# A router that takes its root by log and exp, and experts that fetch their tokens by row: one change to a two-layer transformer kernel

## Chip, core and metric

The kernel runs on one core of a Trainium2 chip. The metric is the device time of one execution in microseconds (us); three runs of the kernel before took 1812.9, 1816.25 and 1819.8, median 1816.25. All data are f32 in DRAM.

## What is computed

One sequence of 512 tokens with 1024 features goes through two blocks. The first has a mixer (a recurrence and attention, with 256 context tokens), then a layer of 16 experts; the second has another mixer and a wide feed-forward layer. The change lies at the seam of the first mixer and the experts. The reference there, cut down:

```python
x = x + g1 * y_x                                  # y_x ends with ... @ w_out
h = modulate(rms_norm(x, norm2_g), sh2, sc2)      # h * (1 + sc2) + sh2
aff = softmax(h @ w_router)                       # 512 x 16
gate, idx = top_k(swapaxes(aff, 1, 2), 64)        # each expert takes its 64 best tokens
xe = h[idx]
hid = silu(xe @ w_gate) * (xe @ w_up)             # per expert, 64 x 1024
ye = (hid @ w_down) * gate
x = x + g2 * zeros_like(h).at[idx].add(ye)
```

Each expert has three weights of 1024 x 1024, so the 16 experts read 201 MB.

## The kernel before

**Tools.** The kernel is written in a tile language: pools hand out buffers by tag and count, and the waits are made from the reads and writes of the tiles. The language also sets the order of the instructions on each engine with a timing model of its own, so an engine's order can differ from the order of the lines; `after` adds an order by hand. A product of f32 operands leaves two records in the trace, a transpose one. The products marked mm3 split f32 into a high and a low part (fp32r) and make three products of them.

**Output projection, mix_out (L937).** w_out is read in four blocks of 256 columns (loop n over wN). For each block and each of the four blocks b of 128 tokens, the result is scaled by g1 and added to X (L966, L967), and the squares of the row are summed on ACT (L968). `logits(n)` transposes two chunks of 128 features of all tokens (L955), scales them by sc2 on ACT (L957) and multiplies them with the router's weights into four accumulators lg (L959). It is called for block n - 1 within block n, and for the last block after the loop.

**Router (L982).** The row sums give 1/rms by `rstd` (L143): a square root on ACT, a reciprocal on DVE. Then a preload of the table for exp, the softmax over 16 columns, a transpose to 16 rows of 512 (L1004), eight rounds of max and match_replace (L1012, L1013) that mark the 64 best, a scan that numbers them (L1016), and a transpose back (L1020). `sl` then holds for each token and expert the slot 1 to 64, or 0.

**Experts, moe (L1024).** The experts go in eight pairs p; the two of a pair use the two halves of the array's columns (64 tokens each), so their products run side by side. Per pair:
- `gemm` (L1074) makes G with w_gate and U with w_up, from xe (chunks of 128 features x 128 chosen tokens); the weights come by `mload`.
- `back(p)` (L1114) makes the one-hot D by comparing iota with sl, transposes it (L1119), rounds it to fp32r as oh, and multiplies D with the affinities (L1124) for the gates gc.
- `prep(p + 1)` (L1097) scales a one-hot by 1/rms and gathers the next pair's tokens as a product of X with it (L1105), 8 chunks x 4 token blocks; the results get sc2 and sh2 on ACT and DVE (L1107, L1110). prep(0) stands before the first gemm.
- silu(G) * U is transposed (L1150), `gemm` makes Y with w_down, Y is scaled by gate and g2 and split in two fp32r parts yh (L1173 to L1175), and each of the four token blocks gets its scatter: two products with oh (L1178, L1179) and one addition on DVE (L1184) to an accumulator ACC. ACC is added to X on POOL at the last pair (L1171), whose scatter goes to X itself. The last pair makes Y in three column parts (`gemm_parts`, L1062).

**Weights.** `mload` (L1035) issues every load on SP's queue, in order; a load waits until its buffer's last reader is done, and the loads behind it wait too. A load is 1 MiB: chunks of 128 rows x 1024 columns, each partition getting pieces of 4 KB. The list `kinds` names the ring of buffers, 15 (x1 six times, raw 3, hl 3 as pairs of halves, x2 3); six more fresh buffers (the tags of rw1 and rw2, and the two of the accumulators) are used once before the ring goes round. The first loads are issued while mix_out runs.

Of the kernel before, what the change touches and what calls it, by code (L numbers as in the profile page):

```python
# [9 lines left out]
F32 = mybir.dt.float32  # L10
# [10 lines left out]
def constants():  # L21
# [31 lines left out]
    iota = np.repeat(np.arange(1, 65, dtype=f)[None, :], 128, axis=0)  # L53
    return {
# [6 lines left out]
    }  # L61

# [6 lines left out]
class Build:  # L69
# [111 lines left out]
    def first_mixer(self):  # L181
# [19 lines left out]
        at = 0  # L201
# [12 lines left out]
        put("n2", I["norm2_g"][0].rearrange("(r p) -> r p", p=128), 8)  # L214
# [12 lines left out]
        nc.vector.tensor_copy(self.pcol, tp[:, :128])  # L227
        cs = p1.tile([128, 8, 32], F32, name="cs")
# [157 lines left out]
        es1.close()  # L386
        esw = ExitStack()
# [20 lines left out]
    def ctx_part(self, cx, rest):  # L408
# [20 lines left out]
        def shift(i):  # L429
            for j, at in enumerate((0, 1, 2, 3)):  # L430
                if at == i:
                    self.mod_col(cx, pc, (self.sh2, self.sc2)[j // 2], 3 + j // 2, j % 2)
# [18 lines left out]
        nc.vector.scalar_tensor_tensor(self.sc2, self.sc2, 1.0, self.c("n2"), op0=ALU.add, op1=ALU.mult)  # L451
# [473 lines left out]
    def mod_col(self, pool, psp, out, wi, half, tag="mr"):  # L925

        nc = self.nc
        for s, row in self.mod_rows(pool, psp, wi, tag, (half,)):
            ps = psp.tile([128, 512], F32, name="mr", tag=tag, bufs=self.nmr)
            for k in range(4):  # L930
                nc.tensor.matmul(ps[:, 2 * k:2 * k + 2], row[:, k * 128:(k + 1) * 128], self.selc,
                                 start=True, stop=True)
            c = 8 * wi + 4 * s
            nc.vector.tensor_tensor(out[:, 4 * s:4 * s + 4], ps[:, :8].rearrange("p (k i) -> p k i", i=2)[:, :, 0],
                                    self.c("bmod")[:, c:c + 4], op=ALU.add)

    def mix_out(self, end):  # L937
# [3 lines left out]
        nc.sync.dma_start(wr, I["w_router"][0].rearrange("(k p) e -> p k e", p=128))  # L941
# [9 lines left out]
        def logits(n):  # L951
            for k in (2 * n, 2 * n + 1):
                tp = pp.tile([128, 512], F32, name="tp", tag="tp", bufs=2)
                for b in range(4):
                    nc.tensor.transpose(tp[:, b * 128:(b + 1) * 128], self.X[:, b, k * 128:(k + 1) * 128], self.ident)  # L955
# [4 lines left out]

        for n, ks in enumerate(self.wN(I["w_out"][0], 0, 1024)):
            s = slice(n * 256, (n + 1) * 256)
            for b in range(4):
# [18 lines left out]
    def router(self):  # L982

        nc, mo, ms, pp = self.nc, self.mo, self.ms, self.pmx
        iota = self.iota = ms.tile([128, 64], F32, name="iota")
        nc.sync.dma_start(iota, self.I["k_iota"])
        rs = self.rs = ms.tile([128, 4], F32, name="rs")
# [3 lines left out]
        e = self.aff = ms.tile([128, 4, 16], F32, name="aff")  # L991
# [32 lines left out]
    def moe(self):  # L1024
# [4 lines left out]
        acc = [(self.mwx2, "acc0"), (self.mwx2, "acc1")]  # L1029
        kinds = ["x1"] * 6 + ["raw"] * self.nraw + ["hl"] * (self.nhl // 2) + ["x2"] * 3  # L1030
        self.tail = False
        todo = (kinds[:6] + [(self.rw1, "rw2"), (self.rw2, "rw")] + kinds[6:] +
                [(self.rw1, "rw"), (self.rw2, "rw2")] + acc)

        def mload(src, last):  # L1035
            if last == 2 and not self.tail:

                self.tail = True
                todo[:] = ["x2", "x2", "x2", (self.rw2, "rw2")] * 3
            if not todo:  # L1040
                todo.extend(k for k in kinds if not last or k != "hl")
            kind = todo.pop(0)
            shape = [128, src.shape[1], src.shape[2]]
# [12 lines left out]
            else:  # L1056
                pool, n = (self.mwx, 6) if kind == "x1" else (ms, 3)
                t = pool.tile(shape, F32, name="mwt", tag="mwt", bufs=n)
# [3 lines left out]
        def gemm_parts(ps, lhs, wa, wb):  # L1062

            ws = [w.rearrange("(k p) f -> p k f", p=128) for w in (wa, wb)]
            for y, c in zip(ps, parts):
                for kk in range(2):
                    tl = [mload(w[:, 4 * kk:4 * kk + 4, c], 2) for w in ws]
# [6 lines left out]
        def gemm(ps, lhs, wa, wb, last=0):  # L1074
            wa = wa.rearrange("(k p) f -> p k f", p=128)
            wb = wb.rearrange("(k p) f -> p k f", p=128)
            for kk in range(4):
                tl = [mload(w[:, 2 * kk:2 * kk + 2, :], last) for w in (wa, wb)]
# [8 lines left out]
        def onehot(p, tag, prev=None):  # L1087
            D = ms.tile([128, 4, 128], F32, name="D", tag=tag, bufs=1)
            ins = nc.vector.tensor_tensor(D.rearrange("p b (a s) -> p b a s", a=2),
                                          self.iota.unsqueeze(1).unsqueeze(1).to_broadcast([128, 4, 2, 64]),  # L1090
                                          self.sl[:, :, 2 * p:2 * p + 2].unsqueeze(3).to_broadcast([128, 4, 2, 64]),
                                          op=ALU.is_equal)
            if prev:
                self.after(ins, prev)
            return D

        def prep(p):  # L1097

            Ds = onehot(p, "Ds")
            nc.vector.tensor_tensor(Ds, Ds, self.rs.unsqueeze(2).to_broadcast([128, 4, 128]), op=ALU.mult)  # L1100
            xe = XE[p % 2]
            for k in range(8):
                ps = self.psmm()[:, :128]
                for b in range(4):
                    nc.tensor.matmul(ps, self.X[:, b, k * 128:(k + 1) * 128], Ds[:, b], start=(b == 0), stop=(b == 3))  # L1105
                if k % 2:
# [581 lines left out]
```

## Time and profile before

| | |
|---|---|
| median of three runs | 1816.25 us (1812.9 to 1819.8) |
| the profiled execution's own time | 1816.96 us |
| its span, first to last instruction | 1815.2 us |
| mean granted clock of TensorE | 0.98 |
| PE, DVE, ACT, POOL busy | 1710.9, 824.7, 655.2, 131.9 us |
| DMA | 327.73 MB, of it 176,480 packets of SP's and ACT's queue |

Times in rows are us from the span's start. PE is TensorE's products, PEld its weight loads, DVE, ACT and POOL the other engines, SPq and ACTq the queues that issue DMAs. L1083 is a line of the kernel file. A busy PE is not PE at its peak, since products are pipelined and their ends modelled. The DMA share is the mean busy share of 16 DMA engines; it can pass 1 a little. In a chain, each piece is the time from its own start to the start of what it released.

### The profile page before, as it was taken

How to read it: one execution, taken by the hardware profiler on the slowest of the kernel's cores; microseconds unless marked ns; L12 is line 12 of the kernel's file. 1: busy time of each engine (PE TensorE's matmuls, PEld its weight loads, DVE VectorE, ACT ScalarE, POOL GpSimd, SP SyncE). 2: the span in 40 equal slices, each digit the busy share in tenths (PEclk: the TensorE clock that was granted, in tenths of full speed). 3: DMA queues.
4: the chain of work that ended last, by engine and by line, in shares of the span. 5: the costliest groups of instructions: out<-in, count | busy, mean ns of one | idle time of the engine just before them, and what ended most of it. 6: DMA issues, size and time to landing. Idle time of an engine off the chain costs nothing.

```text
span 1815.2 us, 26611 instructions
## 1 busy us (share of the span) xinstructions
PE 1710.9 (94%) x11031; PEld 1247.3 (69%) x11031; DVE 824.7 (45%) x1605; ACT 655.2 (36%) x1137; POOL 131.9 (7%) x153
## 2 busy tenths in 40 slices
PE   5999899999999599999999998899999999999999
PEld 3987679666669553444434433697677989898989
DVE  5536885855343511221221221656675543434342
ACT  4638984656432210010000000655563242323131
POOL 0100000122110000000000010410221000000000
PEclk9999999999999799999999999999999999999999
DMA  9562122112458578999999996451002222323231
GB/s 308 184 206 76 48 71 65 60 37 92 168 174 298 210 304 317 409 409 384 393 375 362 407 383 229 131 163 50 22 24 70 83 91 84 115 72 116 71 115 48
DMA packets 177393, 327.73 MB, mean 181 GB/s; under 512 B 8580, under 2 KB 115816, under 8 KB 177272
## 3 DMA queue, kind: packets, MB, share of 16 engines
q1 hardware_dynamic: 176480, 325.44, 49.9%
q8 instruction: 87, 1.43, 0.3%
q10 hardware_dynamic: 744, 0.51, 0.1%
q14 instruction: 34, 0.28, 0.0%
q0 software_dynamic: 48, 0.08, 0.0%
HBM read 323.91 MB, written 2.10 MB: 180 GB/s over the span
## 4 chain that ended last, share of the span: by engine, by line
PE 63%; DVE 4%; DMA 1%; ACT 1%; issue 1%; POOL 0%; SPq 0%; DVEq 0%; ACTq 0%
PE mm L90 10%; PE mm L89 10%; PE mm L91 10%; PE G L1083 7%; PE U L1083 6%; PE Y L1083 5%; PE mm L1105 3%; PE po L1615 1%; PE mm L1178 1%; PE pt L1568 1%; PE mm L1179 1%; PE sc L1547 1%; DMA wraw<-in_w_in_dram 1%; PE sc L1548 1%; PE Y L1071 0%
## 5 line engine op out<-in xcount | busy, mean ns | idle before, releaser
L81 ACT ACTIVATE whi<-wraw 128x1024 fp32r<-128x1024 f32 (+1 forms) x171 | 173.4, 1018 | 365.0 <-PE mm L89 178.2
L83 DVE TENSOR_TENSOR wlo<-wraw,whi 128x1024 fp32r<-128x1024 f32 (+1 forms) x171 | 207.9, 1218 | 110.4 <-ACT whi L81 109.5
L90 PE MATMUL mm<-whi,ul 128*128 128x256 f32 x512 | 144.3, 282 | 0.0
L91 PE MATMUL mm<-whi,uh 128*128 128x256 f32 x512 | 143.2, 281 | 0.0
L89 PE MATMUL mm<-wlo,uh 128*128 128x256 f32 x512 | 143.1, 281 | 0.0
L90 PE MATMUL mm<-HXh,wlo 128*128 128x512 f32 x256 | 102.2, 399 | 1.8 <-DVE wlo L83 1.8
L89 PE MATMUL mm<-HXl,whi 128*128 128x512 f32 x256 | 103.5, 404 | 0.0
L91 PE MATMUL mm<-HXh,whi 128*128 128x512 f32 x256 | 101.2, 395 | 0.0
L89 PE MATMUL mm<-H,whi 128*128 128x512 f32 x256 | 99.7, 390 | 0.0
L91 PE MATMUL mm<-H,whi 128*128 128x512 f32 x256 | 99.6, 389 | 0.0
L90 PE MATMUL mm<-H,wlo 128*128 128x512 f32 x256 | 99.6, 389 | 0.0
L90 PEld LDWEIGHTS mm<-whi,ul 128*128 128x128 f32 x512 | 96.5, 188 | 1.0 <-DVE ul L1651 0.8
L89 PEld LDWEIGHTS mm<-wlo,uh 128*128 128x128 f32 x512 | 96.2, 188 | 0.2
L91 PEld LDWEIGHTS mm<-whi,uh 128*128 128x128 f32 x512 | 96.2, 188 | 0.0
L1105 PEld LDWEIGHTS mm<-D,X 128*128 128x128 f32 x512 | 61.9, 199 | 18.5 <-issue 15.4
L1660 DVE SCALAR_TENSOR_TENSOR X<-mm,r,X 128x256 f32<-128x256 f32 x64 | 30.9, 483 | 88.2 <-PE mm L91 88.2
L1105 PE MATMUL mm<-D,X 128*128 128x128 f32 x512 | 66.7, 288 | 2.8 <-DVE D L1100 1.8
L1148 DVE TENSOR_TENSOR hy<-hy,U 128x1024 f32<-128x1024 f32 x8 | 9.8, 1222 | 124.4 <-PE U L1083 124.4
L1083 PE MATMUL Y<-mwt,xh 128*64 128x512 f32 x240 | 59.9, 594 | 5.4 <-DVE xh L1151 5.4
L1646 DVE TENSOR_SCALAR r<-mm 128x512 f32<-128x512 f32 x32 | 22.1, 692 | 85.2 <-PE mm L91 85.2
L1173 DVE SCALAR_TENSOR_TENSOR hy<-Y,gc,g 128x512 f32<-128x512 f32 (+1 forms) x17 | 11.6, 715 | 106.4 <-PE Y L1083 100.2
L90 PEld LDWEIGHTS mm<-HXh,wlo 128*128 128x128 f32 x256 | 48.4, 189 | 13.8 <-DVE wlo L83 2.6
(539 smaller groups left out, 4073.0 us busy)
## 6 DMA issues: line engine op xcount, KB each, us to landing
mwt<-in_w_exp_gate_dram SPq DMA_DIRECT2D x41, 1024.0 KB, 9.1
mwt<-in_w_exp_up_dram SPq DMA_DIRECT2D x35, 1024.0 KB, 10.6
mwt<-in_w_exp_down_dram SPq DMA_DIRECT2D x33, 1024.0 KB, 13.2
wraw<-in_w_in_dram SPq DMA_DIRECT2D x29, 1024.0 KB, 5.1
wraw<-in_w_mod_dram SPq DMA_DIRECT2D x16, 1024.0 KB, 6.9
wraw<-in_w_up_dram SPq DMA_DIRECT2D x16, 1024.0 KB, 5.6
wraw<-in_w_down_dram SPq DMA_DIRECT2D x16, 1024.0 KB, 5.1
mwh<-in_w_exp_up_dram SPq DMA_DIRECT2D x30, 512.0 KB, 9.2
```

The source lines that it names most:

```text
L81: i1 = self.nc.scalar.activation(hi, src, AF.Copy)
L83: i2 = self.nc.vector.tensor_tensor(lo, src, hi, op=ALU.subtract)
L89: mm(ps, ah, bl, start=first, stop=False)
L90: mm(ps, al, bh, start=False, stop=False)
L91: mm(ps, ah, bh, start=False, stop=last)
L1083: nc.tensor.matmul(ps[64 * a:64 * a + 64, n], lhs[:, k, 64 * a:64 * a + 64], tl[a][k2][:, n * 512:(n + 1) * 512], start=(k == 0), stop=(k ...
L1105: nc.tensor.matmul(ps, self.X[:, b, k * 128:(k + 1) * 128], Ds[:, b], start=(b == 0), stop=(b == 3))
L1178: nc.tensor.matmul(ps, oh[:, b * 128:(b + 1) * 128], yh[:, 1, s], start=True, stop=False)
L1179: nc.tensor.matmul(ps, oh[:, b * 128:(b + 1) * 128], yh[:, 0, s], start=False, stop=True)
L1547: nc.tensor.matmul(sc, QS[:, h, s], KDl[:, br, p // 2, :n], start=True, stop=False)
L1646: nc.vector.tensor_scalar(r, ps, 0.0, None, op0=ALU.max)
L1660: nc.vector.scalar_tensor_tensor(self.X[:, b, s], ps, r2[:, b:b + 1], self.X[:, b, s], op0=ALU.mult, op1=ALU.add)
```

## The change

It has five parts.
1. The chunks of 128 features that the router and the experts use become every second feature of a block of 256 (`chunk`), and weight rows are read two in a row (`(k p j) f`), so each partition of a load gets 8 KB in one piece; the hl halves keep 4 KB. sh2, sc2 and norm2_g are laid out to match: three small loads in place of one, two transposes more (`r256`, `pair`), `mod_col` with strided slices.
2. `last_logits(b)` makes the last block's logits for each token block as its X is done, scaled on DVE. The root is exp(-0.5 log), its table loaded before the loop.
3. X is copied to DRAM (XD) from POOL's queue, a column block at a time. For pairs 1 to 7, `chosen` gets the tokens' numbers and 1/rms from the one-hot's product with the affinities (two columns wider), and POOL issues an indirect DMA of 128 rows of XD; the next pair's is issued when the one at hand has been used. `prep` scales the rows, transposes them and applies sc2 and sh2.
4. The first pair keeps the one-hot product, in four pieces, each before its quarter of G (`first`); its one-hot Dr is made by eight operations on DVE and POOL.
5. The scatter goes to X at once; pairs 0, 2 and 4 are held and scattered with the next, so four products of two pairs meet in PSUM and are added once. The ring has a sixteenth buffer (x3) in place of the accumulators, and the last pair's twelve loads go to other buffers.

```diff
+def chunk(k):
+    return slice(k // 2 * 256 + k % 2, k // 2 * 256 + 256, 2)
...
+        r256 = st.tile([12, 256], F32, name="r256")
+        for i, src in enumerate((I["b_mod"][0, 3072:4096], I["b_mod"][0, 4096:5120], I["norm2_g"][0])):
+            nc.scalar.dma_start(r256[4 * i:4 * i + 4], src.rearrange("(r p) -> r p", p=256))
...
+        def last_logits(b):
...
+            for j in range(2):
+                nc.tensor.transpose(tp[:, j * 128:(j + 1) * 128], self.X[:, b, chunk(6 + j)], self.ident)
+            for j in range(2):
+                nc.vector.tensor_scalar(ht[:, j * 128:(j + 1) * 128], tp[:, j * 128:(j + 1) * 128],
+                                        self.sc2[:, 6 + j:7 + j], None, op0=ALU.mult)
+            for j in range(2):
+                nc.tensor.matmul(self.lg[b], ht[:, j * 128:(j + 1) * 128], wr[:, 6 + j], start=False, stop=(j == 1))
+        self.pre = self.table("natural_log_exp_and_others")
...
-                if n and b == 1:
+                if b == 3:
+                    nc.gpsimd.dma_start(self.XD.rearrange("(b p) f -> p b f", p=128)[:, :, s], self.X[:, :, s])
+                if n and b == (1 if n < 3 else 0):
                     logits(n - 1)
+                if n == 3:
+                    last_logits(b)
...
-        logits(3)
...
-        self.rstd(mo, rs, rs, 1.0 / 1024, 4)
-        pre = self.table("natural_log_exp_and_others")
+        self.after(nc.scalar.activation(rs, rs, AF.Ln, bias=self.eps, scale=1.0 / 1024), pre)
+        nc.scalar.activation(rs, rs, AF.Exp, scale=-0.5)
+        self.aff = ms.tile([128, 4, 18], F32, name="aff")
+        e = self.aff[:, :, :16]
+        nc.gpsimd.tensor_copy(self.aff[:, :, 16], iota[:, 64:])
+        nc.gpsimd.tensor_copy(self.aff[:, :, 17], rs)
...
-        kinds = ["x1"] * 6 + ["raw"] * self.nraw + ["hl"] * (self.nhl // 2) + ["x2"] * 3
+        kinds = ["x1"] * 6 + ["raw"] * self.nraw + ["hl"] * (self.nhl // 2) + ["x2"] * 3 + ["x3"]
...
-                [(self.rw1, "rw"), (self.rw2, "rw2")] + acc)
+                [(self.rw1, "rw"), (self.rw2, "rw2")])
...
-                todo[:] = ["x2", "x2", "x2", (self.rw2, "rw2")] * 3
+                todo[:] = ["x1", "x1", (self.rw2, "rw2"), "x2", "x2", "x2", "x1", "x1", "x1", "x1",
+                           (self.rw2, "rw2"), "x2"]
...
+            ws = [w.rearrange("(k p j) f -> p k j f", p=128, j=2) for w in (wa, wb)]
             for kk in range(4):
-                tl = [mload(w[:, 2 * kk:2 * kk + 2, :], last) for w in (wa, wb)]
+                if before:
+                    before(kk)
+                tl = [mload(w[:, kk], last) for w in ws]
...
+        def weights(p):
+            D = onehot(p, "D")
+            ps = self.psmm()[:, :18]
+            for b in range(4):
+                nc.tensor.matmul(ps, D[:, b], self.aff[:, b], start=(b == 0), stop=(b == 3))
+            g = ms.tile([128, 18], F32, name="gs", tag="gs", bufs=3)
+            nc.vector.tensor_copy(g, ps)
+            return g
+        def chosen(p):
+            if p > 7:
+                return None
+            xg = self.mwx2.tile([128, 1024], F32, name="xg", tag="xg", bufs=1)
+            g = weights(p)
+            at = ms.tile([128, 1], U32, name="at", tag="at", bufs=2)
+            nc.vector.tensor_copy(at, g[:, 16:17])
+            nc.gpsimd.indirect_dma_start(xg, None, self.XD, bass.IndirectOffsetOnAxis(ap=at, axis=0))
+            return xg, g
+        def prep(p, xg, g):
+            nc.vector.tensor_scalar(xg, xg, g[:, 17:18], None, op0=ALU.mult)
             xe = XE[p % 2]
-            for k in range(8):
-                ps = self.psmm()[:, :128]
-                for b in range(4):
-                    nc.tensor.matmul(ps, self.X[:, b, k * 128:(k + 1) * 128], Ds[:, b], start=(b == 0), stop=(b == 3))
...
+            for k0 in range(0, 8, 4):
+                ps = self.psmm()
+                for k in range(k0, k0 + 4):
+                    nc.tensor.transpose(ps[:, (k - k0) * 128:(k - k0 + 1) * 128], xg[:, chunk(k)], self.ident)
...
+        for b in range(4):
+            for a in range(2):
+                (nc.gpsimd if a else nc.vector).tensor_scalar(
+                    Dr[:, b, 64 * a:64 * a + 64], self.iota, self.sl[:, b, a:a + 1], self.rs[:, b:b + 1],
+                    op0=ALU.is_equal, op1=ALU.mult)
+        def first(kk):
+            ps = self.psmm()
+            for j in range(2):
+                for b in range(4):
+                    nc.tensor.matmul(ps[:, j * 128:(j + 1) * 128], self.X[:, b, chunk(2 * kk + j)], Dr[:, b],
+                                     start=(b == 0), stop=(b == 3))
...
-            gemm(G, xe, wg[2 * p], wg[2 * p + 1])
+            gemm(G, xe, wg[2 * p], wg[2 * p + 1], before=None if p else first)
+            if p == 0:
+                gs, ch = weights(0), chosen(1)
...
-            oh, gc = back(p, ins)
+            oh = back(p)
...
-                xe, ins = prep(p + 1)
+                xe = prep(p + 1, *ch)
+                gs, ch = ch[1], chosen(p + 2)
...
+            held.append((oh, yh))
             for y, s in zip(Y, parts):
...
+                if p in (0, 2, 4):
+                    continue
                 for b in range(4):
                     ps = self.psmm()[:, :s.stop - s.start]
-                    nc.tensor.matmul(ps, oh[:, b * 128:(b + 1) * 128], yh[:, 1, s], start=True, stop=False)
-                    nc.tensor.matmul(ps, oh[:, b * 128:(b + 1) * 128], yh[:, 0, s], start=False, stop=True)
...
+                    parts_ = [(o, y[:, i, s]) for o, y in held for i in (1, 0)]
+                    for i, (o, v) in enumerate(parts_):
+                        nc.tensor.matmul(ps, o[:, b * 128:(b + 1) * 128], v, start=(i == 0), stop=(i == len(parts_) - 1))
+                    nc.vector.tensor_tensor(self.X[:, b, s], ps, self.X[:, b, s], op=ALU.add)
```

## Rows read from the trace of the kernel before

**Rows 1.** Windows: length; busy PE, PEld, DVE, ACT, POOL (records); clock, DMA share, GB/s.

```profile
612.80:632.00 19.20, 1.95 (x9) 1.25 (x10) 15.93 (x33) 0.11 (x1) 0.00 (x0) 0.50 0.58 221
...
642.00:694.20 52.20, 50.94 (x278) 23.04 (x276) 6.90 (x13) 5.62 (x9) 0.00 (x0) 1.00 0.81 316
...
694.20:752.40 58.20, 56.93 (x294) 25.70 (x292) 13.58 (x23) 5.31 (x9) 0.00 (x0) 1.00 0.99 386
...
816.00:1080.80 264.80, 249.27 (x1173) 105.28 (x1174) 54.11 (x91) 20.79 (x36) 0.00 (x0) 0.99 0.98 383
```

**Rows 2.** Waits of PE, 640 to 1140: who for whom, us, times, longest.

```profile
PE Y L1071 <- DMA mwt<-in_w_exp_down_dram: 1.3, 2, 0.8
```

**Rows 3.** Windows again, same columns: stretches read for DMA.

```profile
720.00:840.00 120.00, 114.66 (x602) 54.86 (x600) 28.68 (x51) 11.04 (x20) 0.00 (x0) 1.00 1.03 409
...
680.00:700.00 20.00, 19.77 (x88) 6.96 (x89) 4.64 (x8) 1.86 (x3) 0.00 (x0) 1.00 0.69 252
...
25.00:30.00 5.00, 4.83 (x37) 2.53 (x36) 3.66 (x8) 0.00 (x0) 0.00 (x0) 1.00 1.07 346
...
1112.00:1147.24 35.24, 27.04 (x159) 15.31 (x157) 16.86 (x28) 8.47 (x15) 5.54 (x6) 0.98 0.89 275
...
645.39:1098.00 452.61, 430.99 (x2104) 186.43 (x2102) 94.50 (x161) 37.25 (x64) 9.71 (x13) 1.00 0.98 383
```

**Rows 4.** Timeline of PE, first pair: start, us, what, count.

```profile
670.68 7.41 PE L1105 MATMUL mm<-D,X 128*128 128x128 f32 x64
...
677.92 1.04 PE L1150 MATMUL tp<-ca,hy 128*128 128x128 f32 x8
```

**Rows 5.** Chain that ended last, around 630 to 656: start, us, what.

```profile
631.64 10.14 PE mm L1105 x64
...
641.79 13.88 PE G L1083 x64
```

**Rows 6.** Windows of line L1083 alone: length, busy PE, PEld, clock, DMA.

```profile
889.87:918.23 28.36, 18.94 (x66) 4.95 (x64) 1.00 0.87 333
```

**Rows 7.** Windows of line L1105 alone, first pair, same columns.

```profile
669.33:677.92 8.59, 7.24 (x64) 7.22 (x64) 1.00 1.03 409
```

**Rows 8.** Timeline of SP's queue: start, us, DMA issues and their count.

```profile
645.39 3.80 SPq L1059 DMA_DIRECT2D mwt<-in_w_exp_down_dram  x3
...
669.73 29.56 SPq L1059 DMA_DIRECT2D mwt<-in_w_exp_up_dram  x7
...
1131.55 0.47 SPq L1046 DMA_DIRECT2D mwo<-in_w_exp_down_dram  x1
```

**Rows 9.** Timeline of PE in the router.

```profile
607.83 0.44 PE L955 MATMUL tp<-ca,X 128*128 128x128 f32 x2 [0.39 <-DVE X L967]
...
609.00 2.63 PE L959 MATMUL lg<-wr,ht 128*128 128x16 f32 x16 [0.74 <-ACT ht L957]
```

**Rows 10.** Timeline of ACT in the router.

```profile
609.55 1.28 ACT L145 ACT_TABLE_LOAD   x1
```

**Rows 11.** Timeline of DVE in the router.

```profile
608.41 0.17 DVE L988 TENSOR_REDUCE rs<-ssn 128x4 f32<-128x16 f32 x1 [0.64 <-ACT yt L968]
...
611.45 0.66 DVE L993 SCALAR_TENSOR_TENSOR aff<-lg,rs,c16s 128x16 f32<-128x16 f32 x4
...
630.17 0.69 DVE L1089 TENSOR_TENSOR D<-iota,sl 128x512 f32<-128x512 f32 x1
```

**Rows 12.** Timeline of POOL: its one DMA issue of before.

```profile
132.75 0.72 POOL L544 DMA_DIRECT2D levf<-in_k_lev_dram  x1 [51.43 <-PE tp L507]
```

**Rows 13.** DMA issues: what, count, KB each, median us to landing.

```profile
mwo<-in_w_exp_down_dram SPq DMA_DIRECT2D x2, 512.0 KB, 5.7
...
levf<-in_k_lev_dram POOLq DMA_DIRECT2D x1, 80.0 KB, 5.0
```

**Rows 14.** Timeline of PE, end of the experts and start of the second mixer.

```profile
1138.65 0.59 PE L1071 MATMUL Y<-mwo,xh 128*64 128x256 f32 x2
...
1147.24 0.78 PE L89 MATMUL mm<-H3l,whi 128*128 128x512 f32 x1
```

More of the change, by code (lines that the diff above doesn't have):

```diff
@@ L53, in constants @@
     iota = np.repeat(np.arange(1, 65, dtype=f)[None, :], 128, axis=0)
+    token = r[:, None] + 128 * np.arange(4)[None, :]
+    iota = np.concatenate([iota, token.astype(f)], axis=1)
     return {
@@ L227, in first_mixer @@
         nc.vector.tensor_copy(self.pcol, tp[:, :128])
+        tp = pst.tile([128, 512], F32, name="tp", tag="tr", bufs=2)
+        for j in range(2):
+            nc.tensor.transpose(tp[:, 12 * j:12 * j + 12], r256[:, j::2], self.ident[:12, :12])
+        self.pair = p1.tile([128, 2, 12], F32, name="pair")
+        nc.vector.tensor_copy(self.pair, tp[:, :24].rearrange("p (j r) -> p j r", j=2))
         cs = p1.tile([128, 8, 32], F32, name="cs")
@@ L386, in first_mixer @@
         es1.close()
+        dp = self.es.enter_context(tc.tile_pool(name="xd", bufs=1, space=bass.MemoryType.DRAM))
+        self.XD = dp.tile([512, 1024], F32, name="XD")
         esw = ExitStack()
@@ L450, in ctx_part @@
         shift(3)
-        nc.vector.scalar_tensor_tensor(self.sc2, self.sc2, 1.0, self.c("n2"), op0=ALU.add, op1=ALU.mult)
+        pairs = lambda t: t.rearrange("p (k j) -> p k j", j=2)
+        nc.vector.scalar_tensor_tensor(pairs(self.sc2), pairs(self.sc2), 1.0, self.pair[:, :, 8:]
+                                       .rearrange("p j k -> p k j"), op0=ALU.add, op1=ALU.mult)
         nc.scalar.activation(KY, FR, AF.Sigmoid, scale=-1.0)
@@ L923, in mod_bc, with mod_col @@
         return end
-    def mod_col(self, pool, psp, out, wi, half, tag="mr"):
+    def mod_col(self, pool, psp, out, which, half, tag="mr"):
         nc = self.nc
-        for s, row in self.mod_rows(pool, psp, wi, tag, (half,)):
+        for s, row in self.mod_rows(pool, psp, 3 + which, tag, (half,)):
             ps = psp.tile([128, 512], F32, name="mr", tag=tag, bufs=self.nmr)
             for k in range(4):
-                nc.tensor.matmul(ps[:, 2 * k:2 * k + 2], row[:, k * 128:(k + 1) * 128], self.selc,
+                at = k // 2 * 256 + k % 2
+                nc.tensor.matmul(ps[:, 2 * k:2 * k + 2], row[:, at:at + 256 - k % 2:2], self.selc,
                                  start=True, stop=True)
-            c = 8 * wi + 4 * s
-            nc.vector.tensor_tensor(out[:, 4 * s:4 * s + 4], ps[:, :8].rearrange("p (k i) -> p k i", i=2)[:, :, 0],
-                                    self.c("bmod")[:, c:c + 4], op=ALU.add)
+            r = 4 * which + 2 * s
+            nc.vector.tensor_tensor(out[:, 4 * s:4 * s + 4].rearrange("p (k j) -> p k j", j=2),
+                                    ps[:, :8].rearrange("p (k j i) -> p k j i", j=2, i=2)[:, :, :, 0],
+                                    self.pair[:, :, r:r + 2].rearrange("p j k -> p k j"), op=ALU.add)
     def mix_out(self, end):
@@ L1042, in mload @@
             kind = todo.pop(0)
+            if len(src.shape) == 4:
+                pool, tag, n = kind + (None,) if isinstance(kind, tuple) else place[kind]
+                t = pool.tile([128, src.shape[1] * 2, src.shape[3]], F32, name="mwt", tag=tag, bufs=n)
+                for i in range(src.shape[1]):
+                    nc.sync.dma_start(t[:, 2 * i:2 * i + 2], src[:, i])
+                return [t[:, i] for i in range(t.shape[1])]
             shape = [128, src.shape[1], src.shape[2]]
@@ L1056, in mload @@
             else:
-                pool, n = (self.mwx, 6) if kind == "x1" else (ms, 3)
-                t = pool.tile(shape, F32, name="mwt", tag="mwt", bufs=n)
+                pool, tag, n = place[kind]
+                t = pool.tile(shape, F32, name="mwt", tag=tag, bufs=n)
                 nc.sync.dma_start(t, src)
@@ L1117, in back @@
+        def back(p):
+            D = onehot(p, "D")
             ps = self.psmm()
@@ L1164, in moe @@
                 gemm_parts(Y, hT, wd[2 * p], wd[2 * p + 1])
-            yh = self.rw1.tile([128, 2, 1024], F32R, name="yh", tag="rw")
-            if p == 0:
-                ACC = [pl.tile([128, 2, 1024], F32, name="acc", tag=t) for pl, t in acc]
-                ACC = [ACC[b // 2][:, b % 2] for b in range(4)]
-            elif p == 7:
-                for b in range(4):
-                    nc.gpsimd.tensor_tensor(self.X[:, b], self.X[:, b], ACC[b], op=ALU.add)
+            yh = (ms if p % 2 else self.rw1).tile([128, 2, 1024], F32R, name="yh", tag="rw")
+            held.append((oh, yh))
             for y, s in zip(Y, parts):
```

93 lines of the change are left out of this document (47 added, 46 removed).

## The prediction, made before the change was run

> **What bounds it now.** I read the page first, then the busy time of each engine by stretch, PE's waits, SP's queue and PE's order in the expert stage. The page has TensorE busy nearly throughout, which does not say what an edit is worth; the change touches the router and the experts, from 598 to 1147 us, so those stretches decide. There the windows show 52.2 us for the first pair of experts, 58.2 for the second and 264.8/4 = 66.2 for each of the middle four, PE at its full level (granted clock 0.99 to 1.00) and the DMA engines busy beside it, at 383 GB/s in the middle [rows 1]. Two engines are near their ends; which one is it? PE's own waits answer for before: in the whole expert stage it waited 1.3 us for a weight transfer [rows 2]. So PE's order sets the end, and DMA waits for PE to give buffers back. But the margin is thin. From 720 to 840 us the queue ran without a gap at 409 GB/s, share 1.03; over all of 645 to 1098 us it made 383 [rows 3]. It is 6% from its own limit, so what PE saves beyond that is not saved: **after the change the transfers set the end**, and the forecast is a sum of start, bytes and rate.
>
> **PE's new cost per pair.** Removed in seven preparations: 64 records of the product with the one-hot, 7.41 us when run in one piece. Added: eight transposes, at the 1.04 us that the eight of L1150 take [rows 4]. The products for the weights (18 columns instead of 16) stood in back as L1124. The scatter keeps its products and halves its additions on DVE. So the second pair's 58.2 becomes 58.2 - 7.4 + 1.0 = 51.8 us. A second saving is in the order. In the middle pairs the preparation is cut into pieces between G and U: in the 28.36 us from 889.87 stand 66 records of G and U, which in one piece would take 66/64 x 13.88 = 14.3, and the preparation with back's products, 8.6 in one piece [rows 5 to 7]. The other 5.5 us are changes between products on half the array's columns and products on all of them. With eight transposes little is left to cut in. Bounds for a pair: 51.8 (no such price) and 66.2 - 6.4 = 59.8 (the price stays whole).
>
> **DMA's new cost.** Expert weights are 16 x 3 x 4.19 = 201.3 MB. By the list in mload 21 loads of 1 MiB fill fresh buffers before one is reused; the rest is 171 MiB. After, 6 + 2 + 10 + 2 = 20 fill fresh ones, so 172 MiB = 180.4 MB wait for PE's first product. The row fetches add 7 x 128 rows x 4 KB = 3.7 MB: 184.1 MB. The rate: with rows of 4 KB 409 GB/s, with the 1 KB rows of 25 to 30 us 346 [rows 3]. Over 16 engines that is 160 and 47 ns a row, so 37.7 ns per KB and 10 ns per row; on that line a row of 8 KB takes 311 ns, 422 GB/s. Thirteen of the ring's sixteen buffers get 8 KB rows, the hl ones keep 4 KB: 419. No row of before has an 8 KB piece on this queue, so both ends stay, 409 (nothing gained) and 419. I take 415, between them: 443.6 us (450.1 to 439.4). The Trainium skill (DMA: Bandwidth & Descriptors, SWDGE vs HWDGE vs iDMA) prefers packets of at most 4096 B; if the queue cuts an 8 KB row so, the rate is 409 and the forecast 6 us later. The last pair's loads no longer share four buffers in turn; that lets them start sooner, but nothing in this sum waits for it.
>
> **Where the transfers start.** Today they pause when the prefill is full and go on when the first buffers come back, at 645.39 [rows 8], 3.6 us after G's first product at 641.79, which itself stands behind 10.14 us of preparation from 631.64 [rows 5]. Three edits act here.
> (1) Router: the last logits go through transposes, copies on ACT and 2.63 us of products [rows 9]; the square root waits for its table, 1.28 us, and the table for exp is loaded behind it [rows 10]; the affinities start at 611.45 [rows 11]. With log and exp in a table loaded ahead, the row sum that ends at 608.6 [rows 11] gives the root after two activations of about 0.3 (an estimate from the small operations beside it), near 609.3. The last block's logits need, after the transposes' start at 607.83, some 0.4 for these, 0.8 for two scalings on DVE (an estimate; 512 columns took 0.69) and a quarter of the products, 0.7: 609.7. So 1.8 us earlier. The table is now loaded on ACT while the output projection keeps PE busy; without that cover it would cost its 1.28.
> (2) One-hot: two DVE operations between 630.17 [rows 11] and 631.64 become eight short ones on DVE and POOL. There is no such row; I take the same 1.5, bounds 0.7 and 4.
> (3) Only a quarter of the preparation now stands before G's first quarter: 2.5 us instead of 10.14, and about 1 for its copy out. G begins near 629.8 + 3.5 = 633.3, and its first buffers come back 3.6 later, at 637.0. PE has idled before, at a granted 0.50 [rows 1], so I add 1.5: **638.5**. If PE's order keeps all quarters in front, it is 643.6. The other three quarters, 7.6 us, lengthen the first pair on PE while buffers already come back.
>
> **What else the queues carry.** One dip stays: between U and Y of the first pair no buffer comes back, seven loads take 29.56 us to issue [rows 8], and 680 to 700 ran at 252 GB/s [rows 3]: 20 x (1 - 252/409) = 7.7, kept as 8. X's copy to DRAM is 2.1 MB from POOL's queue, 5 us of a queue with gaps (share 0.58 from 612.8 to 632 [rows 1]). A POOL issue took 0.72 us [rows 12] and its data landed within 5.0 [rows 13]. Behind the last copy in POOL's queue stand two small copies into the affinity tile and half of the one-hot; the weights' products need the first only after G, the one-hot comes 18 us later. If DVE's affinities have to wait for the small copies, up to 3 us. A fetch has a whole pair, some 52 us, for its landing. The strided reads of X and of the rows have no row of their own; nothing is taken, up to 1.5 us for the first quarter. At the start two more small loads stand in ACT's queue ahead of the sums of squares, each at most the 0.72 of POOL's issue: 0 to 1.4, taken 0.7.
>
> **The sum.** 638.5 + 443.6 + 8 + 1 (the last pair's 1 and 2 KB rows) = 1091.1 for the last landing. Today that is 1131.55 [rows 8] + 5.7 [rows 13] = 1137.2, and the second mixer's first product starts 10.0 later, at 1147.24 [rows 14]; the work between is the same. So 1101.1 instead of 1147.2: -46.1, and with +0.7 at the start -45.4. Does PE keep up? 633.3 + 7.6 + 8 x 51.8 = 1055, and 8.6 to the mixer's product: 37 us to spare. With the whole price of the order left, the removal alone takes 7 x 6.4 = 45 of the 496.9 us from 641.79 to the last Y at 1138.65 [rows 14]: 633.3 + 7.6 + 452 + 8.6 = 1102, the same end. From the profiled execution's 1816.96 (0.7 over the median): **1772 us**. With both ends of rate and start, 1765 to 1784.
>
> **Rivals.**
> A, buffers still come back too late. PE, though shorter, leaves gaps between its stages as today, and the queue keeps its old mean: 184.1/0.383 = 480.7, last landing 638.5 + 480.7 + 1 = 1120, mixer at 1130, **1801**. For it: 383 holds in the middle four pairs as over the whole [rows 1, 3]. Against: those pairs took 66 us.
> B, no dip, and the longer rows at their full worth: 638.5 + 439.4 + 1 + 10 = 1089, **1760**. For it: the line through two rows. Against: the dip's cause, the ring's size, hardly changes (15 to 16).
> C, slower: the clock. Starved of weights PE would be busy 51.8 of 25.7/0.415 = 61.9 us a pair, with a gap at every load. It decides if the mean granted clock falls under 51.8/62.2 = 0.83 (62.2 is what eight pairs may take from 640.9 to the old 1138.65); at 0.80 a pair takes 64.8, the mixer starts at 1168: **1838**. For it: 0.50 after the router [rows 1]. Against: from 1112 to 1147, with PE busy 27.04 of 35.24 us and waiting for loads, 0.98 was granted [rows 3].
> D, the change doesn't do what it says: the fetch lands so late that each pair waits for it, 6.5 us in seven pairs: **1817**. Against: the 5.0 us of a landing [rows 13].
> The Trainium skill (DMA: Bandwidth & Descriptors, Where 436 GB/s comes from) holds that for loads about 358 GB/s of HBM binds; at that rate 184.1 MB take 514 us and the change is slower. The 409 held for 120 us in this trace speaks against it, and it has no chance of its own.
>
> **Numbers.** Forecast 0.64, A 0.18, B 0.10, C 0.04, D 0.04. Faster by over 0.5% (below 1808; about what a measurement of this kernel can tell) are the forecast, A and B: 0.92. D is no change, 0.04; C slower, 0.04. The range takes in A and most of B: 1757 to 1802.
>
> **What would show it.** Right: a DMA share near 1.03 from 700 us to the end of the weights, and PE with waits for weight transfers, which it hardly has today; the first load after the pause at 637 to 641; pairs of 60 to 63 us in the middle; no table load between the projection and the gate's Silu. Wrong: PE still without such waits and the queue near 380 (A), a clock under 0.9 in the middle (C), PE waiting for fetched rows (D), or loads that go on at 643 or later.

## The result, and the profile after

Four runs of the changed kernel took 1785.02 to 1789.6 us, median 1786.24; four of the kernel before had the median 1816.62. The ratio is 0.9848 (95% interval 0.9831 to 0.9866), and the medians differ by 30 us. The forecast was 1772: the sign and the range were right, and 14 us of the gain are missing. The profiled execution took 1785.77 us, its span is 1784.0, the mean granted clock 0.973.

First the busy time by stretch (columns as in [rows 1]): pair 2, the stretch from 700 to 1060 us that holds most of the experts, pair 4, and 10 us inside pair 4.

```profile
734.30:812.31 78.01, 64.31 (x269) 26.02 (x269) 16.82 (x33) 7.48 (x14) 1.88 (x2) 0.91 1.00 410
700.00:1060.00 360.00, 316.30 (x1393) 125.84 (x1391) 71.45 (x128) 31.54 (x54) 5.20 (x5) 0.95 1.00 410
860.77:941.53 80.76, 64.23 (x270) 27.35 (x268) 17.84 (x34) 7.74 (x14) 2.38 (x2) 0.87 0.96 387
920.00:930.00 10.00, 6.17 (x20) 2.87 (x22) 2.89 (x4) 1.05 (x2) 0.00 (x0) 0.51 0.80 298
```

The queue is faster, 410 GB/s over these 360 us where the kernel before made 387 in the same window. But the pairs are uneven: pairs 2 and 4 take 78.0 and 80.8 us, and inside pair 4 there are 10 us at 298 GB/s with a granted clock of 0.51. Who stopped whom? PE's waits from 633 to 1150 us (who for whom, us, times, longest):

```profile
PE tp L1250 <- DVE hy L1248: 17.1, 6, 6.1
PE mm L1178 <- DVE xg L1173: 13.1, 2, 6.6
```

L1178 are the transposes of a fetched row block xg, L1173 its scaling on DVE, L1248 the product silu(G) * U. Now there is no wait for a weight transfer at all, where before had 1.3 us [rows 2]. PE's, DVE's and POOL's timelines of pair 2 show what happens (start, us, what, count, idle time before and what ended it):

```profile
762.70 3.65 PE L1138 MATMUL U<-mwt,xe 128*64 128x512 f32 x14
772.94 1.34 PE L1178 MATMUL mm<-ca,xg 128*128 128x128 f32 x5 [6.59 <-DVE xg L1173]
...
794.31 1.99 PE L1250 MATMUL tp<-ca,hy 128*128 128x128 f32 x8 [5.37 <-DVE hy L1248]
```

```profile
772.13 0.75 DVE L1173 TENSOR_SCALAR xg<-xg,gs 128x1024 f32<-128x1024 f32 x1 [8.59 <-DMA xg<-XD,at]
...
792.05 0.75 DVE L1173 TENSOR_SCALAR xg<-xg,gs 128x1024 f32<-128x1024 f32 x1 [7.81 <-DMA xg<-XD,at]
...
793.04 1.21 DVE L1248 TENSOR_TENSOR hy<-hy,U 128x1024 f32<-128x1024 f32 x1
```

```profile
762.81 0.94 POOL L1168 DMA_INDIRECT xg<-XD,at  x1 [40.88 <-PE mm L1194]
783.56 0.94 POOL L1168 DMA_INDIRECT xg<-XD,at  x1 [19.80 <-DVE at L1167]
```

The fetch for pair 4 is issued at 762.81 and lands at 772.1; its transposes stand in PE's order inside U of pair 2, right behind the fetch, and PE idles 6.59 us. The next fetch goes out at 783.56, and DVE, in order, stands at its scaling until 792.05. Behind that stands the product silu(G) * U of the pair at hand, so PE idles another 5.37 us. The same happens in pair 4. The kernel's lines ask for one preparation a pair; the language's order, made with its own timing model, pulls two into pairs 2 and 4, and none is left in pairs 3 and 5. What its model took for the landing is not known. SP's queue (start, us) and PE's timeline at the end:

```profile
636.74 6.47 SPq L1112 DMA_DIRECT2D mwt<-in_w_exp_down_dram  x4
...
658.42 3.76 SPq L82 DMA_DIRECT2D wraw<-in_w_exp_gate_dram  x3
...
1057.67 40.58 SPq L1094 DMA_DIRECT2D mwt<-in_w_exp_down_dram  x24
```

```profile
1107.79 1.94 PE L1124 MATMUL Y<-mwt,xh 128*64 128x256 f32 x14
...
1118.64 1.11 PE L1294 MATMUL tp<-ca,X 128*128 128x128 f32 x4 [3.87 <-DVE H3l L1287]
1119.40 0.78 PE L96 MATMUL mm<-H3l,whi 128*128 128x512 f32 x1
```

The last expert load is issued at 1097.6 (the end of the 24 in the third row), and the second mixer's first product stands at 1119.40, where before it stood at 1147.24 [rows 14].

### The profile page after: what moved, and what is told of

The parts are those of the page before. It is cut to its first block, busy times and chain, and to the rows that moved or that the text cites. A ratio compares the mean times of both kernels' runs of the same rounds, so it can differ in the third digit from the quotient of the medians.

```text
span 1784.0 us, 25877 instructions
## 1 busy us (share of the span) xinstructions
PE 1662.4 (93%) x10641; PEld 1210.2 (68%) x10641; DVE 811.7 (45%) x1607; ACT 652.7 (37%) x1135; POOL 138.1 (8%) x166
## 2 busy tenths in 40 slices
DMA packets 159286, 333.46 MB, mean 187 GB/s; under 512 B 8392, under 2 KB 115632, under 8 KB 139840
## 5 line engine op out<-in xcount | busy, mean ns | idle before, releaser
L1138 PE MATMUL Y<-mwt,xh 128*64 128x512 f32 x288 | 66.9, 620 | 4.1 <-issue 2.5
L1248 DVE TENSOR_TENSOR hy<-hy,U 128x1024 f32<-128x1024 f32 x8 | 9.7, 1218 | 127.6 <-PE U L1138 127.6
L1743 DVE TENSOR_SCALAR r<-mm 128x512 f32<-128x512 f32 x32 | 22.1, 692 | 85.2 <-PE mm L98 85.2
L1138 PE MATMUL G<-mwt,xe 128*64 128x512 f32 x240 | 59.4, 598 | 0.0
L97 PEld LDWEIGHTS mm<-HXh,wlo 128*128 128x128 f32 x256 | 48.4, 189 | 13.7 <-DVE wlo L90 2.6
L1138 PE MATMUL U<-mwt,xh 128*64 128x512 f32 x256 | 57.3, 592 | 0.0
L96 PEld LDWEIGHTS mm<-HXl,whi 128*128 128x128 f32 x256 | 48.5, 189 | 12.2 <-issue 1.9
```

The source lines that it names most:

```text
L96: mm(ps, ah, bl, start=first, stop=False)
L97: mm(ps, al, bh, start=False, stop=False)
L1138: nc.tensor.matmul(ps[64 * a:64 * a + 64, n], lhs[:, k, 64 * a:64 * a + 64], tl[a][k2][:, n * 512:(n + 1) * 512], start=(k == 0), stop=(k ...
L1743: nc.vector.tensor_scalar(r, ps, 0.0, None, op0=ALU.max)
```

## The experiments

**Holding the preparation.** One preparation a pair, behind the product silu(G) * U of the pair at hand:

```diff
-            if p < 7:
-                xe = prep(p + 1, *ch)
-                gs, ch = ch[1], chosen(p + 2)
-            nc.vector.tensor_tensor(hs, hs, U, op=ALU.mult)
+            prev = nc.vector.tensor_tensor(hs, hs, U, op=ALU.mult)
...
+            if p < 7:
+                xe = prep(p + 1, *ch, prev)
+                gs, ch = ch[1], chosen(p + 2)
...
-            nc.vector.tensor_scalar(xg, xg, g[:, 17:18], None, op0=ALU.mult)
+            self.after(nc.vector.tensor_scalar(xg, xg, g[:, 17:18], None, op0=ALU.mult), prev)
```

> The preparation of the next pair and the fetch behind it are held until the hidden units of the pair at hand are multiplied on VectorE, one preparation a pair. Theory (transfers set the end of the experts once PE does not stand for a fetch; in the changed kernel two fetch waits make PE late, so that it is 9 us behind the last landing, and cost the queue two dips and the gap at the end): last landing 636.7 + 184.1 MB / 420 GB/s + 10.5 lost before 700 us + 2 = 1087.5, mixer 10 later at 1097.5 in place of 1119.75, so 1764 us (1760 to 1770), with PE now waiting for weights. Rival 1 (PE's order sets the end throughout): the two long pairs shrink from 78 and 81 us to about 58, 1743 to 1748, and still no wait for weights. Rival 2 (the waits were hidden by the queue): only the two dips come back, 7.4 us, 1779.

1774.37 us, ratio 0.9782 (0.9768 to 0.9796): 12 us under the changed kernel, and no later run is measurably faster; but 10 us short of the theory's number, and nearer to the 1779 of rival 2. Its waits, windows (the stretch as above, then pairs 2, 3 and 4) and chain:

```profile
PE U L1138 <- DMA mwt<-in_w_exp_up_dram: 10.1, 9, 1.4
...
PE Y L1138 <- DMA mwt<-in_w_exp_down_dram: 2.8, 3, 1.3
PE G L1138 <- DMA mwh<-in_w_exp_gate_dram: 2.4, 1, 2.4
```

```profile
700.00:1060.00 360.00, 327.68 (x1468) 127.22 (x1466) 71.39 (x129) 31.47 (x56) 4.68 (x5) 1.00 1.02 419
741.02:799.21 58.19, 55.82 (x253) 22.39 (x254) 13.56 (x25) 5.36 (x10) 0.94 (x1) 1.00 1.01 419
799.21:850.89 51.68, 47.86 (x222) 18.34 (x219) 7.85 (x16) 4.38 (x8) 0.94 (x1) 1.00 1.02 418
850.89:912.13 61.24, 55.84 (x253) 22.43 (x254) 14.58 (x26) 5.58 (x10) 0.94 (x1) 1.00 1.02 420
```

```profile
1019.62 19.81 DMA wraw<-in_w_exp_gate_dram
1039.49 12.58 DMA mwh<-in_w_exp_gate_dram
1052.13 19.81 DMA mwt<-in_w_exp_up_dram
1071.99 3.66 PE U L1138 x14
```

No wait for a fetch is left, pairs 2 and 4 take 58.2 and 61.2 us at a full clock, the queue makes 419 GB/s, and PE now waits for weights, 18.8 us in all (six lines, of which three are shown): this is the state that the prediction described. The chain runs over transfers up to the last U at 1071.99, and over PE from there. The two long pairs had taken 39.3 us more than here, but only 12 come back. Pairs 3 and 5, which held no preparation in the changed kernel and took 48.5 and 48.4 us there, now take 51.7 and 62.6; in the latter PE waits 10.5 us for weights, because the transfers are then what is late.

**Rows of 4 KB.** Every load of 1 MiB in two of 512 KiB:

```diff
-                nc.sync.dma_start(t, src)
+                for i in range(2):
+                    nc.sync.dma_start(t[:, i], src[:, i])
```

> Every load of 1 MiB is issued as two of 512 KiB whose rows are 4 KB. Theory: the queue falls from 420 to 409 GB/s, worth 450.1 - 438.3 = 11.8 us in the transfers; since PE's fetch waits set the end of the changed kernel, a part of it shows, about 6 us: 1792 (1787 to 1798). Rival 1 (row length sets the rate and the queue sets the end): 1798. Rival 2 (the rate came from the fewer waits of the queue, not from its rows): 420 stays, 1786.

> Both edits: preparation held until the hidden units are multiplied, and rows of 4 KB. Theory: the transfers set the end here, so the 11.8 us show in full against the kernel with the held preparation alone, about 1776 if that is 1764; the DMA rate in the middle 409. Rival 1 (PE's order sets the end): no difference to it. Rival 2 (row length does not set the rate): no difference, the rate 420.

On the changed kernel 1784.53, ratio 0.9837 (0.9821 to 0.9852): no loss, where 6 us were expected; that is the number of rival 2, but not its rate, for from 700 to 1060 us the queue made 407 GB/s. With the preparation held 1782.45, ratio 0.9827 (0.9812 to 0.9842): 8 us slower than with long rows. Two lines of PE's waits of the first, to be read against those of the changed kernel above, and the window of the second, to be read against the first window of the held preparation:

```profile
PE tp L1254 <- DVE hy L1252: 14.9, 6, 4.9
PE mm L1182 <- DVE xg L1177: 9.7, 2, 4.9
```

```profile
700.00:1060.00 360.00, 322.16 (x1428) 123.17 (x1426) 71.78 (x129) 30.48 (x55) 4.69 (x5) 0.98 1.03 409
```

409 in place of 419 GB/s. The loads are also half as large here; but the kernel before had loads of 1 MiB in rows of 4 KB, and they too moved at 409 [rows 3], so it is the row's length that sets the rate. Without the fetch waits the slower queue costs most of the 11.8 us that the rates give. With them it cost nothing in sum, but two things met there: beside short rows a fetch also landed sooner (7.5 us in the median, 9.0 beside long ones), and the waits of the two lines above fell from 30.2 us to 24.6. How much of the queue's loss was hidden by the waits, and how much was paid back by the faster fetch, these runs do not tell.

**The one-hot product for all pairs.** `prep` as before the change, no fetch:

```diff
-            nc.gpsimd.indirect_dma_start(xg, None, self.XD, bass.IndirectOffsetOnAxis(ap=at, axis=0))
...
+                for b in range(4):
+                    nc.tensor.matmul(ps, self.X[:, b, chunk(k)], Ds[:, b], start=(b == 0), stop=(b == 3))
```

> The row fetch is undone: pairs 1 to 7 are prepared by the product of X with a one-hot again, all else stays (its rows then already hold sums of earlier experts, since the scatter goes to X). Theory: PE's order sets the end again, 6.4 us more a pair, the fetch waits gone: the kernel before less 3.3 of the router and up to 2 of the first pair, 1808 to 1812; no wait for weights, queue near 385 GB/s in the middle. Rival 1 (the gain came from longer rows and the earlier start, the fetch gave back on PE what it saved): 1786. Rival 2 (the fetch's PE saving of 45 us was the whole gain): 1816.

> The kernel of the fourth run again (product with a one-hot for all pairs; its rows already hold sums of earlier experts), for its trace. Theory (TensorE's order sets the end when the fetch is undone): no wait of TensorE for weights and the queue at 380 to 395 GB/s from 700 to 1060 us, 1808 to 1812. Rival (the transfers set the end here too): 415 to 420 GB/s there and waits for weights as with the held preparation.

1810.2 us, ratio 0.9972 (0.9959 to 0.9984), as the theory had it; the kernel's second run took 1809.31. The window of that run:

```profile
700.00:1060.00 360.00, 347.27 (x1692) 157.84 (x1690) 69.04 (x121) 31.12 (x53) 0.00 (x0) 1.00 0.99 402
```

PE is busy 347 of 360 us and never waits for a weight; the queue makes 402, above the expected 380 to 395. Here too the order puts two preparations into pair 4, all 128 records of their products, and none into pair 5; so it was not the fetch that drew them together. By the ratios and 1816 us, the fetch brings 23 us as the language ordered it (0.9972 less 0.9848) and 35 with the preparation held; all other parts together are worth 5 us as long as PE's order sets the end.

**Parts undone, on top of the held preparation.** (a) The four quarters of the first preparation ahead of G; (b) the router of before; (c) the last pair's loads round four buffers; (d) no pair's scatter held:

```diff
-            gemm(G, xe, wg[2 * p], wg[2 * p + 1], before=None if p else first)
+            if p == 0:
+                for kk in range(4):
+                    first(kk)
+            gemm(G, xe, wg[2 * p], wg[2 * p + 1])
...
-                if n == 3:
-                    last_logits(b)
...
+        logits(3)
...
-                todo[:] = ["x1", "x1", (self.rw2, "rw2"), "x2", "x2", "x2", "x1", "x1", "x1", "x1",
-                           (self.rw2, "rw2"), "x2"]
+                todo[:] = ["x2", "x2", "x2", (self.rw2, "rw2")] * 3
...
-                if p in (0, 2, 4):
-                    continue
```

> On top of the held preparation (1774): all four quarters of the first pair's preparation stand before G again. Theory (the transfers carry the end through the loads of the last U): G and the first buffers come 7.6 us later, but then come back faster than the queue can use them, and the gap at 655 to 660 is filled by what is queued, so 3 to 5 us of it are left: 1778 (1777 to 1780). Rival 1 (PE's own order sets the end; the same products, fewer changes between them): 1773 to 1774. Rival 2 (every microsecond of the later start counts): 1782.

> On top of the held preparation (1774): the router as before, with its last logits in one go behind the projection, square root, reciprocal and the table for exp loaded behind them. Theory: 1.9 us from the last X to the affinities become 3.7, and all behind them moves: 1.8 to 3.3 later, 1777 (1776 to 1778). Rival 1 (an earlier router is lost, the queue is full and PE waits for weights later anyway): 1774. Rival 2 (the projection's end, 1.4 us earlier in the changed kernel, is the edit's too): 1777.7.

> On top of the held preparation (1774): the last pair's twelve loads of w_down go round the four buffers of the kernel before; the instructions' order is the same. Theory: the longer list is what let the last landing come some 9 us ahead of the last product; with four buffers the last loads wait for Y's own products, the last landing is again within 2 us of Y's end, and the end is 4 us later (2 to 8): 1778. Rival 1 (nothing in the sum waits for it, as the prediction has it; the end hangs on the last load of U and PE's work behind it): 1774.

> On top of the held preparation (1774): every pair's scatter at once, with twice the additions on VectorE; the same products in more pieces between those of G. Theory: PE waits 17 us for weights, so three more places where products are cut in are paid from these waits: 1774 (1773 to 1776). Rival 1 (PE's order sets the end): three cut-ins at about 2 us, 1780. Rival 2 (loads come later by each cut-in, since buffers do): 1776 to 1778.

1774.45, 1772.77, 1776.01 and 1774.73 us, ratios 0.9783, 0.9784, 0.9796 and 0.9789, each with some 0.0014 to both sides, so that none can be told from the held preparation. (d) came as its theory said, (a) and (b) at the number of rival 1; (c) lies between theory and rival: from the copy of sl, the last load is issued after 465.7 us where it is after 458.7 with the long list, and the mixer starts 15.7 behind it where it is 21.1, so the list brings the loads forward by 7 us and the end by less than 2. Two traces show why (a) and (b) bring nothing. (a) With the split, then without, stretches of 5 us (the queue's GB/s stand last), each against its own start of the one-hot product (631.10 and 631.20):

```profile
640.00:645.00 5.00, 5.00 (x30) 2.73 (x28) 0.41 (x1) 0.46 (x1) 0.00 (x0) 1.00 0.65 224
660.00:665.00 5.00, 5.00 (x26) 1.72 (x24) 0.93 (x4) 0.00 (x0) 1.08 (x1) 1.00 0.32 81
```

```profile
640.00:645.00 5.00, 5.00 (x31) 2.71 (x31) 0.67 (x2) 2.20 (x3) 0.00 (x0) 1.00 0.00 0
645.00:650.00 5.00, 5.00 (x26) 1.72 (x24) 0.00 (x0) 0.00 (x0) 0.00 (x0) 1.00 0.71 261
655.00:660.00 5.00, 5.00 (x30) 2.75 (x28) 1.48 (x6) 1.02 (x1) 0.00 (x0) 1.00 1.02 431
```

In pieces, the first buffers come back 4.5 us earlier, but the six that the ring can use again are spent by 660, and the next waits for U: 81 GB/s. In one piece the queue starts late, then runs at 431, and from 660 to 665 still at 315. From 640 to 700 the first loses 9.5 us against 420 GB/s, the second 8.5. The next load, into a buffer that U frees, is issued at 662.50 with the split and at 661.34 without: the progress of U sets this stretch, not the beginning of G.

(b) In the router alone the new order is the quicker: from the end of the last X to the affinities 1.9 us against 3.7. But in the last block of the projection the additions to X (DVE's timeline) come at 591.61, 598.08, 602.03 and 605.93 in the changed kernel and at 591.59, 597.39, 600.31 and 603.16 with the router of before: the transposes and products of the last logits cost 2.8 us there. What the edit saves behind the projection it spends inside it, and 1 us more.

**The last pair's G and U ahead of pair 6's Y**, and their loads; then the same with (a) and (b):

```diff
+            late.append((p, hT, oh, gc, held))
+            if p != 6:
+                for a in late:
+                    finish(*a)
+                late = []
```

> On top of the held preparation (1774): the last pair's G and U, and their loads, stand ahead of pair 6's Y. Theory (the end hangs on the last load of the last U, with 38 us of TensorE's work behind it, while the loads behind it need only 20): with eight more loads behind that U the rest of TensorE's work is covered, the end follows the last landing by some 10 us, and 9 us are gained: 1765 (1763 to 1769). Rival 1 (the last landing or the rate alone sets the end): 1774. Rival 2 (TensorE's own work sets it; the next pair's preparation is no longer behind a Y, 3 us more): 1777.

> The same, with the router of the kernel before and the first pair's preparation in one piece. Theory: the last logits cost 2.8 us inside the last block of the projection and give back 1.8 behind it, so going back gains 1; the pieces of the first preparation gained nothing: 1763 to 1765, that is 0 to 2 under the run above. Rival (both edits carry their weight once the tail is covered): 1.8 and 5 us more, 1770 to 1772.

1777.03, ratio 0.9794 (0.9778 to 0.9811), and 1775.88, ratio 0.9786 (0.977 to 0.9802): nothing gained, the theory of the tail falls; the first is at the number of its rival 2, the second at neither of its two. In the first of them the last U ends at 1050.5, as meant, and the last load is issued at 1086.2, but the mixer's first product comes 22.1 later, at 1108.32: the last Y and two scatters, now in one piece behind the loads, keep PE busy from 1075 to 1100 with no wait over 0.6 us. (`finish` holds Y and the scatter of a pair.) What sets the tail is PE's own work on the last weights.

**The router's weights in rows of 64 bytes** (PE waits 2.9 us for them before, 0.6 after):

```diff
+        for j in range(2):
+            nc.sync.dma_start(wr.rearrange("p (k j) e -> p k j e", j=2)[:, :, j],
+                              I["w_router"][0].rearrange("(k p j) e -> p k j e", p=128, j=2)[:, :, j])
```

> On top of the held preparation (1774): the router's weights are loaded in two transfers of 64-byte rows, as short as before, in place of one of 128-byte rows. Theory: TensorE again waits about 2.9 us for them at 550 us, in place of 0.7, and the projection ends 2 to 3 us later. Rival (that wait is a matter of the run, not of the rows): 0.7 as in the other runs.

The wait stayed at 0.6: the length of the rows is not it. Why before waited longer stays open; there is one profile of it.

## Why the prediction was right, and where it failed

**The bound was named rightly, but the change as ordered does not reach it.** "After the change the transfers set the end" needs PE to keep up, and the sum gave it 37 us to spare. Its terms held nearly: with the preparation held, PE is busy 48 to 56 us a pair in pairs 1 to 6, a little under the 51.8 to 59.8, and pairs 4 to 6 take 61.2, 62.6 and 59.9 with their waits for weights. The changed kernel shows the prediction's signs of both sides: the queue's share near 1.00 and no table load before the gate's Silu, but also PE without waits for weights and with waits for fetched rows. What failed is the sentence "a fetch has a whole pair, some 52 us, for its landing". That is the order of the kernel's lines; the instructions stood otherwise in two pairs, and the section on the tools ahead of the prediction says that they can. So rival D came in part: two stalls and their echo on DVE, 24.5 us of PE's time, in place of 6.5 in each of seven pairs. The evidence against it, a landing within 5.0 us [rows 13], was of 80 KB where the queues had room (229 GB/s); here a fetch of 512 KB takes 9.0 (median of seven; the shortest, 5.8, was issued in a gap of the queue). The Trainium skill (DMA: Bandwidth & Descriptors, Queues, rings and completion order) has each DMA engine go round the queues and finish a whole packet of one before the next. The 9.0 us beside rows of 8 KB and 7.5 beside rows of 4 KB agree with that; no run here tests it further.

**The sum, term by term.** The last load was to be issued at 1091.1 - 5.7 = 1085.4 and the mixer to start 15.7 behind it, as before (1147.24 - 1131.55 [rows 8, 14]).

| term | forecast | measured |
|---|---|---|
| first load after the pause | 638.5 | 636.7 |
| rate, GB/s | 415 | 410; 419 with the preparation held |
| lost near the first pair, us | 8 | 7.3 (640 to 700, against 420) |
| issue of the last load | 1085.4 | 1097.6 |
| from there to the mixer | 15.7 | 21.8 |
| from there to the end of the span | 668.0 | 664.6 |

The last three carry the miss: 12.2 + 6.1 - 3.4 - 0.7 (the start-up, which the forecast adds by itself) = 14.2, which is 1785.77 less the 1771.6 forecast for a profiled execution. The 12.2 are the fetch waits: with the preparation held the last load is issued at 1088.8 in an execution whose first G stands 3.7 us later, that is at 1085.1. That this is almost the forecast's 1085.4 is partly luck: a rate of 419 in place of 415 alone would have brought it 4.2 us forward. The 6.1 are the step "the work between is the same": before, the last loads went round four buffers and came so late that PE's work on the last Y was done beside them; with the longer list they come earlier, and PE's work behind them is longer by nearly as much (21.1 us with the preparation held, 15.7 with the old list on top). Nor was what stood between them work alone. The chain of the kernel before reaches the mixer over the load of the mixer's own first weights, next on the queue behind the last expert load (start, us, what):

```profile
1132.67 10.29 DMA wraw<-in_w_in_dram
```

With the old list on the held preparation the chain runs over that load again, 10.26 us; with the long list it runs over PE's last products and no transfer. The prediction saw that the list lets loads start sooner and said that nothing in its sum waits for it; the 15.7 of the sum did. The 3.4 lie behind the mixer's first product and were not traced; other runs of the same lines took 665.0 to 667.3 us there, so most of them may be the execution.

**Start.** 636.7 was nearly right, for partly wrong reasons and with some luck: runs with the same router lines reach the copy of sl at 625.9 to 631.0 us, and this execution was there at 626.6. The router's 1.8 is there to a tenth (1.9 against 3.7 us), and the 2.8 in the projection were overlooked: "a quarter of the products" was counted behind the projection, and the other three quarters, moved into PE's busiest stretch, at nothing. The one-hot took 0.8 from sl to the first product, not 1.5. The 5 us by which the split was to bring the loads forward were worth nothing, as (a) shows: the step looked at the first buffer and not at the seventh.

**Rate.** The line through two rows was good: it gave 422 GB/s for rows of 8 KB and 419 for the ring, and 419 was measured. I took 415. The profile has 19,446 packets of 8 KB or more (159,286 less 139,840), that of the run with short rows 119. The Trainium skill (DMA: Bandwidth & Descriptors, SWDGE vs HWDGE vs iDMA) prefers packets of at most 4096 B, in its table on what GpSimd builds. For these loads, which go by SP's queue, the trace does not bear out that longer ones are cut or slower.

**The other rivals.** A gave 1801 with the queue at 383: it made 410, and 387 in pair 4. B, with the longer rows' full worth and no dip, gave 1760: the rate was its, the dip was not. C wanted a mean granted clock under 0.83: it was 0.95 from 700 to 1060. But the clock did fall to its lower level (1.2 GHz) in the stalls: 0.50 was granted from 770 to 775 us and from 795 to 800, where PE had idled 6.59 and 5.37 us and begun again. Pairs 2 to 5 hold the same four preparations in both orders, and PE is busy 218.2 us in them here and 210.1 with the preparation held: a stall cost its idle time and then slow products, some 4 us for each of the two long pairs.

## What to carry to other kernels

A transfer that is "fetched a pair ahead" in the source has that lead only if the instructions keep it: read the engines' order around the issue and the use, and on every in-order engine what stands behind the waiting instruction. Where two engines are within some per cent of each other, undoing a part says little until the larger wait is gone: long rows were worth nothing in one order, where they also slowed the fetches that PE waited for, and 8 us in the other. An earlier first buffer, or work moved out of a serial stretch, is a gain only if the next buffer comes too, and if the place it is moved to has room.

## What the runs showed of the hardware

Rows of 8 KB moved at 419 GB/s where rows of 4 KB moved at 409, the latter in loads of 512 KiB and of 1 MiB alike. A fetch of 128 rows took 9.0 us in the median beside a full queue of 8 KB rows and 7.5 beside 4 KB rows (8.5 and 7.4 with the preparation held); the shortest of the changed kernel, 5.8, was issued while the queue moved 25 GB/s (655 to 660 us). And executions of the same instructions reach the end of the router (the copy of sl) at 625.9 to 631.0 us, so single profiles were compared from there: from sl to the mixer it is 517.3 us before, 492.8 after, 479.8 with the preparation held, and 478.7 to 481.4 with parts (a) to (d) undone.
